# Down-projection products copied out of PSUM and summed in DRAM by adding transfers

## The chip, the cores and the metric

One Trainium2 chip, one of its NeuronCores. The metric is the device time of one execution in microseconds, as the median of several executions; lower is better. The kernel before takes 2646.35 us (median of 3 runs, 2646.03 to 2647.65).

## The reference, cut to what matters

One decoder layer on 512 tokens of width 2048, everything in float32. A mixing stage (a gated linear recurrence beside an RWKV-7 recurrence) is followed by the part that the change touches, a gated feed-forward block with 6144 hidden channels, and then by a gated embedding and a final norm:

```python
u = rmsnorm(h, ln_ffn[i])
gate = causal_dwconv(u @ w_gate[i], conv_f_w[i], conv_f_b[i])     # 512x2048 @ 2048x6144, 3 taps over time
h = h + (jax.nn.gelu(gate) * (u @ w_up[i])) @ w_down[i]           # 512x6144 @ 6144x2048

u = rmsnorm(h, ln_ple[i])
e = jax.nn.sigmoid(u @ w_ple_gate[i]) * (p[i] @ w_ple_proj[i])
h = h + rmsnorm(e, ln_ple_post[i])
return rmsnorm(h, ln_final)
```

## The kernel before, in words

Every large product is done in three passes of a reduced float32 format: each operand is split into a high part, made by a ScalarE copy, and a low part, made by a VectorE subtraction of the high part from the original, and the three products high x high, high x low and low x high are summed in PSUM. Weights arrive through a queue of 512 KB pieces (`wfill_`): SyncE issues the load into a raw buffer (`wraw`, or `hw0` to `hw4` for the down-projection), ScalarE makes `whi` (L127), VectorE makes `wlo` (L128). There are three pairs of `whi` and `wlo`, so a pair is made while TensorE is still at the unit two places ahead of its own. The hidden activations are split by `split` in the same way, high part by ScalarE (L140), low part by VectorE (L141).

`phase2` works through the feed-forward block in 12 chunks of four hidden tiles of 128 channels. For each hidden tile f, `gate_up` runs the gate product and then the up product, in two halves of 24 matmuls each (L1212 to L1214). The gate leaves PSUM by VectorE (L1234), goes through the convolution over time (ScalarE L1236, twice VectorE L1238), the activation (ScalarE L1239) and a scaling on GpSimd (L1240); when the up product is done, VectorE multiplies it in (L1245) into a raw hidden tile (`hw5`, `hw6`). After four tiles, `hidden` forms the chunk's operands.

The down-projection of the first 11 chunks saves an eighth of the multiplications: for each column block b (two of 512 columns in each half of the outputs) it forms seven products i = 0 to 6 of sums of weight quarters and sums of hidden quarters, where plain blocking takes eight. A product is 2 token tiles (tt) by 6 matmuls into two PSUM banks (L1294 to L1296); six banks are shared by these. Its result must be added, with a sign, to one or more of four quarters of the residual stream `h3`, which lies in SBUF as 16 tiles of 128 tokens by 512 columns (number 4 x token tile + column block). In the kernel before, VectorE adds each result straight from PSUM (L1309): to `h3`, or to two running sums in SBUF, `qx` and `qz`, that several quarters share (`ADDS` says which). At the end of the eleventh chunk twenty VectorE additions (L1348) put `qx` and `qz` into `h3`. The last chunk is done by eight plain products (`down_last`, four column blocks, two halves of the hidden channels), added at L1320; after each column block TensorE turns the stream's tiles (`to_features`, L1333) for the next stage. The order of units is written out in `ffn_order`: between products of chunk c stand the gate and up halves of chunk c + 1, so that at the end the last products of chunk 11 lie among the halves of the last hidden tile, f = 47, and `down_last` begins right after its up product.

The instructions of each engine stand in one queue that is fixed at build time. A list scheduler with priorities places them by its own model of durations; at run time each engine takes its queue in order and waits at an instruction until its semaphores are there. The tags of a pool (`T(tag, bufs)`) name buffers that are reused in turn, and an instruction that writes one waits until the last reader of its former content is done.

Of the kernel before, what the change touches and what calls it, by code (L numbers as in the profile page):

```python
# [4 lines left out]
F32 = mybir.dt.float32  # L5
F32R = mybir.dt.float32r
AF = mybir.ActivationFunctionType
ALU = mybir.AluOpType
# [4 lines left out]
S = 512  # L13
# [7 lines left out]
NF = FF // 128  # L21
FC = 4
# [63 lines left out]
class Builder:  # L86
# [1084 lines left out]
    def phase2(self):  # L1171
        nc, A, k2 = self.nc, self.A, self.k2
        V, SC, G, TE = nc.vector, nc.scalar, nc.gpsimd, nc.tensor
        self.MM = 6
        self.auxtag = ("wk", 2)
        T = lambda tag, bufs=1, shape=(128, S), dt=F32: self.t(k2, tag, shape, dt, bufs)
# [22 lines left out]
        h3 = [self.bp.tile([128, S], F32, tag="x%s%d" % ("hl"[i // 8], i % 8), name="h3_%d" % i, bufs=1) for i in range(16)]  # L1199
# [54 lines left out]
        def hidden(last):  # L1254
# [12 lines left out]
            if last:  # L1267
# [14 lines left out]
            return o  # L1282


        qx, qz = (T(n, 1, (128, 2, 2, 512)) for n in ("qx", "qz"))
        st = lambda th, nh: lambda tt, b: h3[(2 * th + tt) * 4 + 2 * nh + b]
        QX, QZ = lambda tt, b: qx[:, tt, b], lambda tt, b: qz[:, tt, b]
        ADDS = [[(QX, ALU.add), (st(0, 0), ALU.add)], [(QZ, ALU.add)], [(QX, ALU.add)], [(st(0, 1), ALU.add)],
                [(st(1, 1), ALU.subtract), (st(1, 0), ALU.add)], [(st(0, 0), ALU.add)], [(st(1, 0), ALU.add)]]

        def product(ps, x, w, tt, first, last):
            ts_ = slice(tt * 128, (tt + 1) * 128)
            for k in range(2):
                TE.matmul(ps, x[0][:, k, ts_], w[0][:, k, :], start=first and k == 0, stop=False)  # L1294
                TE.matmul(ps, x[0][:, k, ts_], w[1][:, k, :], start=False, stop=False)  # L1295
                TE.matmul(ps, x[1][:, k, ts_], w[0][:, k, :], start=False, stop=last and k == 1)  # L1296

        def down(ch, b, i):
            w = self.wnext()
            ps = [self.mm(), self.mm()]  # L1300
            for tt in range(2):
                product(ps[tt], self.hids[ch][i], w, tt, True, True)
            for at, op in ADDS[i]:
                for tt in range(2):
                    o = at(tt, b)
                    if ch == 0 and i < 2 and at in (QX, QZ):
                        SC.activation(o, ps[tt], AF.Copy)
                    else:
                        V.tensor_tensor(o, o, ps[tt], op)  # L1309

        def down_last(cb, kh):
            if kh == 0:
                self.pd = [self.mm() for tt in range(4)]
            w = self.wnext()
            for tt in range(4):
                product(self.pd[tt], self.hids[NF // FC - 1][kh][tt // 2], w, tt % 2, kh == 0, kh == 1)
            if kh == 1:
                for tt in range(4):
                    h = h3[tt * 4 + cb]
                    V.tensor_tensor(h, h, self.pd[tt], ALU.add)  # L1320
# [17 lines left out]
        for o in self.ffn_order():  # L1338
            if o[0] == "g":
                gate_up(*o[1:])  # L1340
            elif o[0] == "q":
                down(*o[1:])
                if o[1:] == (NF // FC - 2, 1, 6):
                    for b in range(2):
                        for q, at, op in ((QX, st(1, 0), ALU.add), (QX, st(0, 1), ALU.subtract), (QZ, st(0, 1), ALU.add),
                                          (QX, st(1, 1), ALU.subtract), (QZ, st(1, 1), ALU.add)):
                            for tt in range(2):
                                V.tensor_tensor(at(tt, b), at(tt, b), q(tt, b), op)  # L1348
            else:
                down_last(*o[1:])  # L1350
                if o[2] == 1:
                    to_features(o[1])
# [13 lines left out]
            self.split(t_[:, 0], t_[:, 1], r)  # L1366
            px.append((t_[:, 0], t_[:, 1]))
        rsh = k2.tile([128, 4], F32, name="rsh")
        hq = [T("q" + n, 1, (128, 2, 512)) for n in "xz"]
        ss = k2.tile([128, 20], F32, name="ss")  # L1370

        sg2, sb = (k2.tile([128, 20], F32, name=n) for n in ("sg2", "sb"))
        se, sge, sbe, ssh = (k2.tile([128, 4], F32, name=n) for n in ("se", "sge", "sbe", "ssh"))
        MU, AD = ALU.mult, ALU.add
# [80 lines left out]
        for cb in range(4):  # L1455
            ph, pl = self.wnext()
            p2 = [T("hw%d" % (6 + i), 1, (128, 2, 512)) for i in range(2)]
            pp = [p2[tt // 2][:, tt % 2] for tt in range(4)]
            for tt in range(4):
                ps = self.mm()  # L1460
                ts_ = slice(tt * 128, (tt + 1) * 128)
                for k in range(2):
                    TE.matmul(ps, px[k][0][:, ts_], ph[:, k, :], start=k == 0, stop=False)
                    TE.matmul(ps, px[k][0][:, ts_], pl[:, k, :], start=False, stop=False)
                    TE.matmul(ps, px[k][1][:, ts_], ph[:, k, :], start=False, stop=k == 1)
                SC.activation(pp[tt], ps, AF.Copy)
            if cb == 0:
                t_ = k2.tile([128, 4], F32, name="rsp")
                V.tensor_reduce(ssh.unsqueeze(2), ss3.rearrange("p (t c) -> p t c", c=4), mybir.AxisListType.X, ALU.add)
                V.tensor_scalar(t_, ssh, 1.0 / D, RMS_EPS, ALU.mult, ALU.add)  # L1470
                G.tensor_tensor(t_, t_, self.mhalf[:, 0:4], ALU.pow)
                V.tensor_scalar(rsh, t_, 0.5, None, ALU.mult)
            n, w = (8, 512) if cb < 3 else (4, 256)
            pg = [self.mm()[:, 0:w] for tt in range(4)]
            for u in range(n):
                kk = KT // n
                gate(pg, range(4), [self.wnext()], range(u * kk, u * kk + kk), u == 0, u == n - 1)
                if cb == 3 and u == 1:
                    us = [self.wnext(), self.wnext()]
            for tt in range(4):  # L1480
                embed(tt, cb, gated(tt, pg[tt], slice(0, w)), pp, slice(0, w))
                post(tt, cb, slice(0, w))
                if cb == 3:

                    SC.activation(hq[tt // 2][:, tt % 2, 0:256], h3[tt * 4 + 3][:, 256:512], AF.Copy)
                    V.tensor_tensor(pp[tt][:, 0:256], pp[tt][:, 256:512], gpost[3][:, 256:512], MU)
                gain(tt, cb)
        early()
# [3 lines left out]
        with self.tc.manual_schedule(engines={ET.PE, ET.DVE, ET.Activation, ET.Pool}):  # L1492
            for tt in range(4):
                pg = {tt: self.mm()[:, 0:256]}
                for u in range(5):
                    if u == len(us):
                        us.append(self.wnext())
                    k = 2 * u if u < 2 else 4 * u - 4
                    gate(pg, [tt], us[u:u + 1], range(k, KT), u == 0, u == 4)

                sg, ee, x = T("tmp", 2), T("tmp", 2), e[tt * 4 + 3][:, last]
                n5 = slice(tt * 5 + 4, tt * 5 + 5)
                SC.activation(sg[:, last], pg[tt], AF.Tanh, scale=rsh[:, tt:tt + 1])
                V.scalar_tensor_tensor(ee[:, last], sg[:, last], 1.0, pp[tt][:, last], AD, MU)
                SC.activation(ee[:, last], ee[:, last], AF.Square, accum_out=ss[:, n5])
                V.scalar_tensor_tensor(x, sg[:, last], 1.0, pp[tt][:, 0:256], AD, MU)
                SC.activation(sg[:, 0:256], x, AF.Square, accum_out=sg2[:, n5])
                V.scalar_tensor_tensor(ee[:, 0:256], hq[tt // 2][:, tt % 2, 0:256], 2.0, x, MU, MU, accum_out=sb[:, n5])
# [12 lines left out]
            for cb in range(4):  # L1521
                final(3, rf, cb, cb < 3)
# [67 lines left out]
```

## Time and profile before

| | |
|---|---|
| Time, median of 3 runs | 2646.35 us |
| Lowest and highest | 2646.03 and 2647.65 us |
| Span of the profiled execution, first to last instruction | 2643.4 us |
| What lies around it (median less span) | 2.95 us |
| TensorE matmuls busy | 2601.4 us, 98% of the span |
| VectorE busy | 1721.3 us, 65% |
| ScalarE busy | 1081.7 us, 41% |
| GpSimd busy | 219.4 us, 8% |
| Moved by DMA | 265.56 MB, 100 GB/s in the mean |
| Mean granted TensorE clock | 0.993 |

Busy shares are means over the whole span. Matmuls overlap each other in the pipeline, so a busy TensorE isn't yet one at its peak, but where it is busy in every slice no other engine can delay it there. All transfers of this kernel are issued by SyncE; GpSimd issues none, so this trace holds no row of its queue. In the rows, PE is TensorE, PEld its weight load, DVE is VectorE, ACT ScalarE, POOL GpSimd and SP SyncE; SPq is SyncE's issue of a transfer.

### The profile page before, as it was taken

To read this page: it belongs to the slowest core of one execution; us is meant where nothing else is said; L and a number is where in the kernel's file an instruction comes from. 1 tells how busy PE (TensorE), PEld (TensorE's weight loads), DVE (VectorE), ACT (ScalarE), POOL (GpSimd) and SP (SyncE) were. 2 spreads that over 40 slices of the span, in tenths; PEclk is the share of its full clock that TensorE was granted. 3 is DMA by queue.
4 is the path that set the end of the run, shared out by engine and by line. 5 is a ranking of instruction groups with operands and counts; after the bars stand their busy time and mean duration, and the time that the engine had idled before them with its cause. 6 is when DMAs were issued, how large, how long until landed. Compare 5 with 4: busy or idle time off the path is not lost.

```text
span 2643.4 us, 43548 instructions
## 1 busy us (share of the span) xinstructions
PE 2601.4 (98%) x18466; PEld 2133.7 (81%) x18466; DVE 1721.3 (65%) x2420; ACT 1081.7 (41%) x1515; POOL 219.4 (8%) x177
## 2 busy tenths in 40 slices
PE   9989999999999999999999999999999999999997
PEld 8867778777877888888888888888888888888887
DVE  5764776667666535666676676666666667775447
ACT  6563555546433433333333333333333333335335
POOL 0010000101122300000000000000000000000001
PEclk9999999999999999999999999999999999999999
DMA  7222222222243323223232323323332332332223
GB/s 250 92 69 66 93 77 68 79 79 90 93 129 128 105 87 104 96 97 110 97 104 94 106 95 101 107 96 106 101 105 97 103 104 96 104 108 88 96 92 108
DMA packets 84483, 265.56 MB, mean 100 GB/s; under 512 B 9792, under 2 KB 12480, under 8 KB 84288
## 3 DMA queue, kind: packets, MB, share of 16 engines
q1 hardware_dynamic: 84288, 262.78, 30.1%
q8 instruction: 144, 2.36, 0.4%
q14 instruction: 51, 0.42, 0.1%
HBM read 254.62 MB, written 8.13 MB: 99 GB/s over the span
## 4 chain that ended last, share of the span: by engine, by line
PE 69%; DVE 2%; ACT 1%; issue 1%; POOL 0%; DMA 0%; POOLq 0%; ACTq 0%; DVEq 0%
PE wk L1212 12%; PE wk L1213 12%; PE wk L1214 12%; PE mm L1296 6%; PE mm L1295 6%; PE mm L1294 6%; PE mm L1385 2%; PE mm L1387 2%; PE mm L1386 2%; PE mm L157 2%; PE mm L161 2%; PE mm L159 2%; PE mm L1212 1%; PE mm L1214 1%; PE mm L1213 1%
## 5 line engine op out<-in xcount | busy, mean ns | idle before, releaser
L127 ACT ACTIVATE whi<-wraw 128x1024 fp32r<-128x1024 f32 (+1 forms) x361 | 373.8, 1035 | 746.9 <-PE mm L159 205.8
L128 DVE TENSOR_TENSOR wlo<-wraw,whi 128x1024 fp32r<-128x1024 f32 (+1 forms) x361 | 440.5, 1220 | 207.6 <-ACT whi L127 201.6
L1212 PE MATMUL wk<-uh,whi 128*128 128x512 f32 x1408 | 547.8, 389 | 0.0
L1213 PE MATMUL wk<-ul,whi 128*128 128x512 f32 x1408 | 547.7, 389 | 0.0
L1214 PE MATMUL wk<-uh,wlo 128*128 128x512 f32 x1408 | 547.7, 389 | 0.0
L127 ACT ACTIVATE whi<-hw 128x1024 fp32r<-128x1024 f32 x154 | 163.3, 1061 | 464.6 <-PE wk L1213 414.4
L157 PE MATMUL mm<-xh,whi 128*128 128x512 f32 x832 | 332.6, 400 | 0.9 <-DVE hT L447 0.9
L161 PE MATMUL mm<-xh,wlo 128*128 128x512 f32 x832 | 332.5, 400 | 0.0
L159 PE MATMUL mm<-xl,whi 128*128 128x512 f32 x832 | 330.9, 398 | 0.0
L1214 PEld LDWEIGHTS wk<-uh,wlo 128*128 128x128 f32 x1408 | 264.4, 188 | 54.8
L1212 PEld LDWEIGHTS wk<-uh,whi 128*128 128x128 f32 x1408 | 264.4, 188 | 54.7
L1213 PEld LDWEIGHTS wk<-ul,whi 128*128 128x128 f32 x1408 | 264.4, 188 | 54.7
L128 DVE TENSOR_TENSOR wlo<-hw,whi 128x1024 fp32r<-128x1024 f32 x154 | 188.7, 1225 | 181.5 <-ACT whi L127 179.1
L1295 PE MATMUL mm<-wlo,hid 128*128 128x512 f32 x680 | 265.1, 390 | 0.0
L1296 PE MATMUL mm<-whi,hid 128*128 128x512 f32 x680 | 264.9, 390 | 0.0
L1294 PE MATMUL mm<-whi,hid 128*128 128x512 f32 x680 | 264.8, 389 | 0.0
L1240 POOL TENSOR_TENSOR tmp<-tmp,rsa 128x512 f32<-128x512 f32 x48 | 87.2, 1818 | 1361.1 <-ACT tmp L1239 1361.1
L157 PEld LDWEIGHTS mm<-xh,whi 128*128 128x128 f32 x832 | 157.4, 189 | 36.4 <-issue 3.0
L161 PEld LDWEIGHTS mm<-xh,wlo 128*128 128x128 f32 x832 | 157.2, 189 | 34.4 <-issue 1.9
L159 PEld LDWEIGHTS mm<-xl,whi 128*128 128x128 f32 x832 | 157.3, 189 | 33.7 <-issue 1.8
L1309 DVE TENSOR_TENSOR h<-h,mm 128x512 f32<-128x512 f32 x264 | 175.0, 681 | 0.6
L1295 PEld LDWEIGHTS mm<-wlo,hid 128*128 128x128 f32 x680 | 127.7, 188 | 26.3
(514 smaller groups left out, 3592.1 us busy)
## 6 DMA issues: line engine op xcount, KB each, us to landing
wraw<-wgu SPq DMA_DIRECT2D x192, 512.0 KB, 3.2
hw<-wd SPq DMA_DIRECT2D x88, 512.0 KB, 3.3
wraw<-wz SPq DMA_DIRECT2D x80, 512.0 KB, 3.6
wraw<-wpg SPq DMA_DIRECT2D x31, 512.0 KB, 3.2
wraw<-wo SPq DMA_DIRECT2D x22, 512.0 KB, 3.4
wraw<-wo SPq DMA_DIRECT2D x20, 256.0 KB, 3.0
tmp<-xT SPq DMA_DIRECT2D x16, 256.0 KB, 2.7
wraw<-wd SPq DMA_DIRECT2D x8, 512.0 KB, 3.2
```

Of the source, the lines that this page charges most:

```text
L127: nc.scalar.activation(hi, raw, AF.Copy)
L128: nc.vector.tensor_tensor(lo, raw, hi.bitcast(F32), ALU.subtract)
L157: nc.tensor.matmul(ps, hi[:, k, :], xh, start=first and i == 0, stop=False)
L159: nc.tensor.matmul(ps, hi[:, k, :], xl, start=False, stop=False)
L161: nc.tensor.matmul(ps, lo[:, k, :], xh, start=False, stop=last and i == n - 1)
L1212: TE.matmul(ps, wh[:, k, :], xh, start=h + k == 0, stop=False)
L1213: TE.matmul(ps, wh[:, k, :], xl, start=False, stop=False)
L1214: TE.matmul(ps, wl[:, k, :], xh, start=False, stop=h == 1 and k == 7)
L1294: TE.matmul(ps, x[0][:, k, ts_], w[0][:, k, :], start=first and k == 0, stop=False)
L1295: TE.matmul(ps, x[0][:, k, ts_], w[1][:, k, :], start=False, stop=False)
L1296: TE.matmul(ps, x[1][:, k, ts_], w[0][:, k, :], start=False, stop=last and k == 1)
L1309: V.tensor_tensor(o, o, ps[tt], op)
```

## The change

The two running sums are gone. Each product now has partial sums of its own in DRAM: 28 tiles `pacc`, one for each product i, token tile tt and column block b. ScalarE copies every product from PSUM into one of 8 SBUF buffers `pl` (L1321), and GpSimd's queue sends it to DRAM, for the first chunk as a plain store (L1323), after that as a transfer that adds to what is there (L1325): 308 copies and 308 transfers. For each column block b a new function `combine` loads the 14 partial sums back on GpSimd's queue (L1293), again into `pl` buffers, and VectorE joins them to the stream in 22 additions (L1289). `combine(0)` is called in the eleventh chunk after product 3 of column block 1, `combine(1)` after product 6, the last. The `pl` buffers take the room that `qx` and `qz` had; four of them hold the copies `hq` later on.

```diff
-        qx, qz = (T(n, 1, (128, 2, 2, 512)) for n in ("qx", "qz"))
-        st = lambda th, nh: lambda tt, b: h3[(2 * th + tt) * 4 + 2 * nh + b]
-        QX, QZ = lambda tt, b: qx[:, tt, b], lambda tt, b: qz[:, tt, b]
-        ADDS = [[(QX, ALU.add), (st(0, 0), ALU.add)], [(QZ, ALU.add)], [(QX, ALU.add)], [(st(0, 1), ALU.add)],
-                [(st(1, 1), ALU.subtract), (st(1, 0), ALU.add)], [(st(0, 0), ALU.add)], [(st(1, 0), ALU.add)]]
+        pacc = [[[self.dp.tile([128, S], F32, name="pacc%d_%d_%d" % (i, tt, b)) for b in range(2)] for tt in range(2)] for i in range(7)]
+        st = lambda th, nh, tt, b: h3[(2 * th + tt) * 4 + 2 * nh + b]
+
+        def combine(b):
+            add = lambda o, x, op=ALU.add: V.tensor_tensor(o, o, x, op)
+            for tt in range(2):
+                p = [T("pl", 8) for i in range(7)]
+                for i in (0, 2, 5, 1, 4, 6, 3):
+                    nc.gpsimd.dma_start(p[i], pacc[i][tt][b])
+                c00, c10, c01, c11 = (st(th, nh, tt, b) for nh in range(2) for th in range(2))
+                add(c00, p[0])
+                add(c00, p[5])
+                add(p[0], p[2])
+                add(p[1], p[0], ALU.subtract)
+                add(c10, p[4])
+                add(c10, p[6])
+                add(c10, p[0])
+                add(c01, p[3])
+                add(c01, p[1])
+                add(c11, p[4], ALU.subtract)
+                add(c11, p[1])
...
-            for at, op in ADDS[i]:
-                for tt in range(2):
-                    o = at(tt, b)
-                    if ch == 0 and i < 2 and at in (QX, QZ):
-                        SC.activation(o, ps[tt], AF.Copy)
-                    else:
-                        V.tensor_tensor(o, o, ps[tt], op)
+            for tt in range(2):
+                o = T("pl", 8)
+                SC.activation(o, ps[tt], AF.Copy)
+                if ch == 0:
+                    G.dma_start(pacc[i][tt][b], o)
+                else:
+                    G.dma_start(pacc[i][tt][b], o, accum_op=ALU.add)
...
                 down(*o[1:])
+                if o[1:] == (NF // FC - 2, 1, 3):
+                    combine(0)
                 if o[1:] == (NF // FC - 2, 1, 6):
-                    for b in range(2):
-                        for q, at, op in ((QX, st(1, 0), ALU.add), (QX, st(0, 1), ALU.subtract), (QZ, st(0, 1), ALU.add),
-                                          (QX, st(1, 1), ALU.subtract), (QZ, st(1, 1), ALU.add)):
-                            for tt in range(2):
-                                V.tensor_tensor(at(tt, b), at(tt, b), q(tt, b), op)
+                    combine(1)
...
-        hq = [T("q" + n, 1, (128, 2, 512)) for n in "xz"]
+        hq = [T("pl", 8) for tt in range(4)]
```

Up to the end of the first chunk's gate and up products the queues of all engines are the same. What the scheduler makes of the end of the block is shown at four places. In these rows a name is followed by a number that tells its uses apart, `h` is a tile of the stream, `mm` and `wk` are PSUM banks, `par` holds convolution weights.

VectorE, from the last multiplication of the up product (L1245, tile f = 47) to the low parts of the last two hidden operands (L141, `hid`). Before:

```order
L1348 TENSOR_TENSOR h_13_10678<-h_13_10678,qx_10681 128x512
L1245 TENSOR_TENSOR hw_3207_20658<-tmp_20765,wk_20792 128x512
L128 TENSOR_TENSOR wlo_20919<-wraw_20916,whi_20918 128x1024
L141 TENSOR_TENSOR hid_20905<-hw_3207_20658,hid_20904 128x512
L141 TENSOR_TENSOR hid_20909<-hw_3207_20658,hid_20908 128x512
L128 TENSOR_TENSOR wlo_20949<-wraw_20946,whi_20948 128x1024
```

After, the end of that stretch; between L1245 and the first row here stand two weight splits and ten further additions of L1289:

```order
L1289 TENSOR_TENSOR h_13_10678<-h_13_10678,pl_21478 128x512
L1289 TENSOR_TENSOR h_5_10670<-h_5_10670,pl_21479 128x512
L1289 TENSOR_TENSOR pl_21474<-pl_21474,pl_21476 128x512
L1289 TENSOR_TENSOR h_13_10678<-h_13_10678,pl_21480 128x512
L1289 TENSOR_TENSOR pl_21475<-pl_21475,pl_21474 128x512
L1289 TENSOR_TENSOR h_13_10678<-h_13_10678,pl_21474 128x512
L1289 TENSOR_TENSOR h_7_10672<-h_7_10672,pl_21477 128x512
L1289 TENSOR_TENSOR h_15_10680<-h_15_10680,pl_21478 128x512
L1289 TENSOR_TENSOR h_7_10672<-h_7_10672,pl_21475 128x512
L1289 TENSOR_TENSOR h_15_10680<-h_15_10680,pl_21475 128x512
L141 TENSOR_TENSOR hid_21539<-hw_3505_21198,hid_21538 128x512
L141 TENSOR_TENSOR hid_21543<-hw_3505_21198,hid_21542 128x512
```

Before, one weight split stands between L1245 and the two L141; now two weight splits and all but two of `combine(1)`'s 22 additions do.

GpSimd, after, where `combine(0)` begins (before, there is no row at all between the scalings of tiles 46 and 47). In `pacc` the three numbers are token tile, column block and a serial number; the product's own number isn't printed:

```order
L1293 DMA pl_21225<-pacc_0_0_10681 128x512
L1325 DMA pacc_1_1_10696<-pl_21222 128x512
L1293 DMA pl_21227<-pacc_0_0_10689 128x512
L1293 DMA pl_21230<-pacc_0_0_10701 128x512
L1293 DMA pl_21226<-pacc_0_0_10685 128x512
L1293 DMA pl_21229<-pacc_0_0_10697 128x512
L1293 DMA pl_21231<-pacc_0_0_10705 128x512
L1293 DMA pl_21228<-pacc_0_0_10693 128x512
L1293 DMA pl_21250<-pacc_1_0_10683 128x512
L1293 DMA pl_21252<-pacc_1_0_10691 128x512
L1293 DMA pl_21255<-pacc_1_0_10703 128x512
L1293 DMA pl_21251<-pacc_1_0_10687 128x512
```

The first row loads the partial sum 0 of the first token tile, the third to eighth the products 2, 5, 1, 4, 6 and 3; then comes the second token tile with its products 0, 2, 5 and 1 (its 4, 6 and 3 follow). Seven loads of a token tile take seven of the eight `pl` buffers. So of the second token tile only the load of partial sum 0 has a buffer that no addition must free first; its partial sum p takes the buffer that p - 1 of the first token tile had, and the load stands in the queue until the last addition that reads that one is done. The next copies of products (`pl_21324` and those after it in the ScalarE rows below) take the buffers of the second token tile in the same way, and the loads of `combine(1)` those of these copies and of each other.

GpSimd, around the scaling of tile f = 47 (L1240). Before, the queue holds nothing but such scalings and, after them, small powers:

```order
L1240 TENSOR_TENSOR tmp_20304<-tmp_20304,rsa 128x512
L1240 TENSOR_TENSOR tmp_20524<-tmp_20524,rsa 128x512
L1240 TENSOR_TENSOR tmp_20765<-tmp_20765,rsa 128x512
L1471 TENSOR_TENSOR rsp<-rsp,mhalf 128x4
L1418 TENSOR_TENSOR tl_22792<-tl_22790,mhalf 128x1
```

After:

```order
L1325 DMA pacc_0_1_10706<-pl_21443 128x512
L1293 DMA pl_21449<-pacc_0_1_10682 128x512
L1325 DMA pacc_1_1_10708<-pl_21446 128x512
L1293 DMA pl_21451<-pacc_0_1_10690 128x512
L1293 DMA pl_21454<-pacc_0_1_10702 128x512
L1240 TENSOR_TENSOR tmp_21361<-tmp_21361,rsa 128x512
L1293 DMA pl_21450<-pacc_0_1_10686 128x512
L1293 DMA pl_21453<-pacc_0_1_10698 128x512
L1293 DMA pl_21455<-pacc_0_1_10706 128x512
L1293 DMA pl_21452<-pacc_0_1_10694 128x512
L1293 DMA pl_21474<-pacc_1_1_10684 128x512
```

The scaling now stands behind the store of the very last product (the third row) and two loads; eleven loads follow it, of which five are shown.

ScalarE, at the same tile's convolution and activation (L1236, L1239). Before:

```order
L1236 ACTIVATE tmp_20765<-row_10663,par 128x512
L140 ACTIVATE hw_3357_21374<-ld_21372 128x512
L127 ACTIVATE whi_20795<-wraw_20793 128x1024
L1239 ACTIVATE tmp_20765<-tmp_20765 128x512
L127 ACTIVATE whi_20825<-wraw_20823 128x1024
```

After:

```order
L1321 ACTIVATE pl_21324<-mm_21310 128x512
L140 ACTIVATE hw_3691_22008<-ld_22006 128x512
L127 ACTIVATE whi_21395<-wraw_21393 128x1024
L1321 ACTIVATE pl_21327<-mm_21311 128x512
L1321 ACTIVATE pl_21386<-mm_21372 128x512
L1321 ACTIVATE pl_21389<-mm_21373 128x512
L127 ACTIVATE whi_21425<-wraw_21423 128x1024
L1321 ACTIVATE pl_21443<-mm_21429 128x512
L1236 ACTIVATE tmp_21361<-row_10663,par 128x512
L127 ACTIVATE whi_21501<-wraw_21499 128x1024
L1321 ACTIVATE pl_21446<-mm_21430 128x512
L1239 ACTIVATE tmp_21361<-tmp_21361 128x512
```

The copies of the products 4, 5 and 6 of the last chunk's second column block (six `pl` rows) now stand between the weight splits. The copy of the very last one (`pl_21446`, which the GpSimd store above sends) stands behind this tile's L1236, and so behind the VectorE instruction L1234 that L1236 reads.

More of the change, by code (lines that the diff above doesn't have):

```diff
@@ L1483, in phase2 @@
                 if cb == 3:
-                    SC.activation(hq[tt // 2][:, tt % 2, 0:256], h3[tt * 4 + 3][:, 256:512], AF.Copy)
+                    SC.activation(hq[tt][:, 0:256], h3[tt * 4 + 3][:, 256:512], AF.Copy)
                     V.tensor_tensor(pp[tt][:, 0:256], pp[tt][:, 256:512], gpost[3][:, 256:512], MU)
@@ L1507, in phase2 @@
                 SC.activation(sg[:, 0:256], x, AF.Square, accum_out=sg2[:, n5])
-                V.scalar_tensor_tensor(ee[:, 0:256], hq[tt // 2][:, tt % 2, 0:256], 2.0, x, MU, MU, accum_out=sb[:, n5])
+                V.scalar_tensor_tensor(ee[:, 0:256], hq[tt][:, 0:256], 2.0, x, MU, MU, accum_out=sb[:, n5])
                 V.tensor_tensor(x, x, gfin[3][:, last], MU)
```

## The prediction

> **What bounds the kernel now.** I read the page first, then the windows by stage, the list of waits, and the rows of every engine at the end of the feed-forward block. The page's totals, TensorE's waits after 770 us (engine, producer: us, times, longest), and one window from the last short waits to the end of TensorE's dense work (busy time of PE, PEld, DVE, ACT and POOL, granted clock, DMA share, GB/s):
>
> ```profile
> PE 2601.4 (98%) x18466; PEld 2133.7 (81%) x18466; DVE 1721.3 (65%) x2420; ACT 1081.7 (41%) x1515; POOL 219.4 (8%) x177
> ...
> PE mm L157 <- DVE hT L447: 0.9, 1, 0.9
> ...
> 900.00:2620.00 1720.00, 1720.00 (x7808) 1430.94 (x7807) 1111.03 (x1362) 602.79 (x753) 95.35 (x54) 1.00 0.29 99
> ```
>
> TensorE is busy for all of these 1720 us, at full clock, and waits for nobody. The change leaves the matmuls as they are. So whatever it takes off VectorE is worth nothing; at most the 0.9 us of that one wait could be won. And any stall put into this window moves the end by its own length.
>
> TensorE's own times at the end of the block (start, us of one matmul): the units of 12 matmuls of a product (L1294) and of 24 of a gate or up half (L1212).
>
> ```profile
> 2335.82 0.39 PE L1294 MATMUL mm<-whi,hid 128*128 128x512 f32 x1
> 2343.97 0.39 PE L1294 MATMUL mm<-whi,hid 128*128 128x512 f32 x1
> 2346.70 0.39 PE L1212 MATMUL wk<-uh,whi 128*128 128x512 f32 x1
> 2376.61 0.39 PE L1294 MATMUL mm<-whi,hid 128*128 128x512 f32 x1
> 2387.50 0.82 PE L1333 MATMUL wk<-con,h 128*128 128x128 f32 x6
> ```
>
> A product and a half take 8.15 us (2335.82 to 2343.97), so a matmul 0.2264 to 0.2268 us: 12 are 2.72, 24 are 5.44. Product 3 of column block 1 ends at 2346.70. After it: half, product 4 (from 2352.14), half (2354.86), product 5 (2360.30), half of the up product (2363.0), product 6 (2368.45), half (2371.2), `down_last` from 2376.61. Of `down_last` the scheduler now puts 48 matmuls first that need no low part of the last hidden operands: TensorE asks for that low part (L141) at 2376.61 + 48 x 0.2268 = 2387.50. That is the appointment which matters.
>
> **Steady state, eleven chunks: nothing.** The groups (count | busy us, mean ns | idle) of the additions out of PSUM and of a ScalarE copy out of PSUM, and the weight split that stands behind such work:
>
> ```profile
> L1309 DVE TENSOR_TENSOR h<-h,mm 128x512 f32<-128x512 f32 x264 | 175.0, 681 | 0.6
> L1309 DVE TENSOR_TENSOR qx<-qx,mm 128x512 f32<-128x512 f32 x84 | 57.0, 682 | 0.3
> L1309 DVE TENSOR_TENSOR qz<-qz,mm 128x512 f32<-128x512 f32 x40 | 25.5, 677 | 0.0
> ...
> 2346.89 1.06 ACT L127 ACTIVATE whi<-wraw 128x1024 fp32r<-128x1024 f32 x1 [1.88 <-DVE h L1309]
> ...
> 2348.10 1.22 DVE L128 TENSOR_TENSOR wlo<-wraw,whi 128x1024 fp32r<-128x1024 f32 x1
> 2349.24 0.69 DVE L1348 TENSOR_TENSOR h<-h,qx 128x512 f32<-128x512 f32 x1
> ...
> 2357.89 1.29 DVE L1348 TENSOR_TENSOR h<-h,qx 128x512 f32<-128x512 f32 x2
> 2359.09 1.29 DVE L1348 TENSOR_TENSOR h<-h,qz 128x512 f32<-128x512 f32 x2
> ...
> L1307 ACT ACTIVATE qx<-mm x4: 577/580/598, 1023.6 to 1077.9; 128x512 f32<-128x512 f32 x4
> ```
>
> VectorE loses 388 additions (L1309) and 20 (L1348), each 0.60 apart (two from 2357.89 to 2359.09), and gets 44 (L1289): some 218 us less, on an engine that nobody waits for. ScalarE gets 308 copies for 8, by 0.58 us 174 us more: two in 8.15 us. The pair split at 2348.10 to 2349.24 is for the half that starts at 2354.86: 5.6 us of cover, and two copies are 1.2. If that cover were gone, TensorE would wait by what goes beyond.
>
> GpSimd gets 308 transfers of 256 KB, two in 8.15 us. No row shows its issue. Bounds per transfer, a: SyncE's issue from below, GpSimd's own pass over such a tile from above (a row of L1245 stands here too); SyncE's loads of the same 256 KB from DRAM (KB, median us from issue to landing) give the rest of the way:
>
> ```profile
> 2367.38 0.33 SPq L1364 DMA_DIRECT2D ld<-pT  x1
> ...
> 2365.25 1.55 POOL L1240 TENSOR_TENSOR tmp<-tmp,rsa 128x512 f32<-128x512 f32 x1 [33.81 <-ACT tmp L1239]
> ...
> 2376.89 0.69 DVE L1245 TENSOR_TENSOR hw<-tmp,wk 128x512 f32<-128x512 f32 x1 [1.96 <-PE wk L1214]
> ...
> lx<-oa SPq DMA_DIRECT2D x3, 256.0 KB, 2.7
> row<-oa SPq DMA_DIRECT2D x3, 256.0 KB, 2.9
> ```
>
> a lies between 0.33 and 1.55; neither row is nearer in kind (one is an issue by another engine, the other no issue at all), so I take the middle, 0.94. Landing after the issue: 2.8 less 0.33, 2.5 us. A `pl` buffer is then back 0.58 + 0.94 + 2.5 = 4 us after its copy begins; eight buffers are four products, 32.6 us. DMA's share, 0.29, rises: 64 GB/s of stores and as much read back, at the window's 99 GB/s for 0.29, is about 0.38 more. The scaling L1240 now stands behind transfers; it ended at 2366.80 and is read by L1245 at 2376.89: 10 us of cover against two issues, 1.9. None of the three shows on TensorE.
>
> **The end of the block: four round trips.** What the additions need must be loaded, into buffers that the additions themselves free. The rows of before for the instructions on the way:
>
> ```profile
> 2360.49 0.69 DVE L1234 TENSOR_TENSOR row<-wk,rsa 128x512 f32<-128x512 f32 x1
> 2361.28 0.81 ACT L1236 ACTIVATE tmp<-row,par 128x512 f32<-128x512 f32 x1
> ...
> 2377.68 1.23 DVE L128 TENSOR_TENSOR wlo<-wraw,whi 128x1024 fp32r<-128x1024 f32 x1
> 2378.82 1.28 DVE L141 TENSOR_TENSOR hid<-hw,hid 128x512 fp32r<-128x512 f32 x2
> ...
> 2377.61 1.15 ACT L140 ACTIVATE hid<-hw 128x512 fp32r<-128x512 f32 x2
> ```
>
> A split counts 1.14 (2377.68 to 2378.82), an addition 0.60.
>
> 1. `combine(0)`, first token tile. Weight split 2346.89 + 1.06, copy 0.58: product 3 leaves at 2348.53. GpSimd sends it and issues the loads of partial sums 2 and 5: 3a, 2351.35; landed 2353.85. From there VectorE has nine additions (the third to the eleventh) and two splits, 5.40 + 2.28: 2361.53. The later loads arrive under these.
> 2. Second token tile. Its loads wait for buffers, the first of them for that last addition. Loads 2, 5, 1, 4: 4a, and 2.5: 2367.79. Ten additions and two splits, 6.00 + 2.28: 2376.07. The splits belong to product 6, wanted at 2368.45 and ready at 2369.53, and to the half behind it: TensorE waits 1.1 and 0.2, and would begin `down_last` at 2377.9.
> 3. Only now do ScalarE's next copies have a buffer, and only now comes L1234 (2360.49 before). ScalarE: two copies 1.16, split of `down_last`'s first weights 1.06: 2378.29; VectorE's half 1.14: TensorE begins at 2379.43, 1.5 late. ScalarE goes on: copy 0.58, L1236 0.81, split 1.06, copy of the last product 0.58: 2381.32. GpSimd: store and two loads 3a, then L1240 1.55: 2385.69 (2366.80 before). The second load lands at 2385.70, one addition, L1245 0.69, the high parts 1.15: 2388.14, where TensorE, after 24 matmuls, has waited 3.3.
> 4. `combine(1)`. Loads 1, 4, 6, 3 stand behind L1240: 4a and 2.5, 2391.95; four additions and a split 3.54: 2395.49. This frees the second tile's buffers: 4a and 2.5, 2401.75; ten additions 6.0 and L141 1.28: 2409.03.
>
> Against the appointment at 2387.50 that is 21.5 us; the smaller waits above are contained in it, and the last one is about 13 us.
>
> What a wait of TensorE costs beyond itself shows earlier in the trace (windows as above; the row before them has the idle time in brackets):
>
> ```profile
> 188.46 0.48 PE L772 MATMUL wk<-AR,ktl 64*64 64x128 f32 x2 [5.21 <-DVE ktl L705]
> ...
> 186.80:188.40 1.60, 0.00 (x0) 0.00 (x0) 1.60 (x1) 0.00 (x0) 1.06 (x1) 0.50 0.55 223
> 188.40:193.80 5.40, 5.34 (x37) 4.24 (x37) 2.01 (x4) 2.91 (x6) 0.11 (x1) 0.54 0.02 3
> 193.80:196.00 2.20, 2.20 (x45) 1.65 (x44) 0.93 (x3) 0.00 (x0) 0.00 (x0) 1.00 0.00 0
> ```
>
> Idle from 183.25, the clock stood at 0.50 by 186.8, and at 0.54 for 5.4 us after work had begun again: 5.4 x 0.46 = 2.5 us lost. The 13 us wait brings that once; the waits of up to 3.3 us are shorter than the 3.5 us after which it is seen.
>
> The sum stands on the profiled execution, whose span 2643.4 and 2.95 around it are the median of 2646.35: 2646.35 + 21.5 + 2.5 = **2670.3**. Bounds, the same walk: a = 0.33 gives 13.4, with the clock 2662.2; a = 1.55 gives 35.5, with two losses of clock (product 6 then waits 6.8 us too) 2686.9.
>
> The Trainium skill, "TensorE: Matmul & The Clock Gate", Part 1: The HAM clock gate, halves the rate after an idle window of about 3.4 us and restores it after about 3.4 us of sustained work; the fall agrees with the row, the return took longer here. By the page 1.7 us would stand for 2.5, and the sum would be 2669.6. Its "DMA: Bandwidth & Descriptors", Anatomy of one DMA — SWDGE (gpsimd) path, gives 2.0 us + bytes / 436e3, for 256 KB 2.6 us in all, an estimate that leaves 1.7 us behind an issue of 0.94; no row of GpSimd's queue can confirm it here. By it the walk gives 18.3 and the sum 2667.2.
>
> **Rivals.**
> - *GpSimd's issue is slow* (a of 1.2 and more, or landings near 4 us beside the weight loads). For it: the engine's pass over 256 KB takes 1.55. Against: it need not touch the data. 27 to 35 us and one or two clock losses: 2676 to 2687. Chance 0.18.
> - *It is cheap as SyncE's* (a below 0.5): 13.4 to 15 and 2.5, 2662 to 2664. Chance 0.12.
> - *The queue bounds the steady state.* An adding transfer reads and writes DRAM; the share leaves room, but no row shows one. It decides from 8.15 / 2 = 4.08 us per transfer; at 5 us each of 140 later products costs 1.85 more: 259 us, 2905. Chance 0.05.
> - *Not slower: the sums cost nothing.* If the transfers were all hidden, VectorE's own queue would still hold twenty additions and two splits between L1245 and L141; the walk with free transfers ends 6.5 us late, with the clock 9.0, 2655.4. It takes additions of 0.50 us as well, and a clock that holds, to come to 4.0 us, 2650.4. The quoted additions, 0.60 apart, speak against it. Chance 0.05, of it 0.02 for a gain.
>
> **Numbers.** My forecast (a of 0.5 to 1.2: 15 to 26 us, 2664 to 2675) has the remaining 0.60; the time is its middle. From 2660 to 2687 lies this, nearly all of the first rival and most of the second. 0.2% is 5.3 us, about what a measurement tells from no change: slower 0.95, same 0.03, faster 0.02.
>
> **What would show it.** PE stays at 200 of 200 us in windows before 2340. Near its end an idle stretch of about 13 us before a matmul of L1312, released by VectorE's L141, with the clock at a half behind it, and one of about 3 before `down_last`'s L1310. L1289's idle time is put down to DMA, in four clusters; L1234 of the last tile starts near 2376 and L1240 ends near 2386. GpSimd's issue near 0.94 us. I am wrong if TensorE waits in earlier chunks (a copy of ScalarE, a `pl` buffer), if L1289 never waits for a load, or if the time lies at one place that the walk doesn't pass.

## The result: 2871 us, and the profile after

| | before | after |
|---|---|---|
| Time, median | 2647.0 us | 2871.39 us (2862.16 to 2878.46) |
| Ratio | | 1.0848, 95% interval 1.0829 to 1.0866 |
| Span of the profiled execution | 2643.4 us | 2873.7 us |
| TensorE busy | 2601.4 us | 2641.7 us |
| TensorE's waits after 900 us | none | 189.7 us |

The kernel became 224 us slower. The range of the prediction ended at 2687. The engines' totals on the page:

```profile
PE 2641.7 (92%) x18466; PEld 2153.6 (75%) x18466; DVE 1504.6 (52%) x2056; ACT 1232.8 (43%) x1815; POOL 471.2 (16%) x513
```

The list of TensorE's waits from 900 us on (us in total, times, longest):

```profile
PE wk L1212 <- DVE hw L1245: 127.1, 9, 18.2
PE mm L1311 <- DVE wlo L128: 30.1, 4, 23.2
PE mm L1310 <- ACT hid L140: 17.6, 1, 17.6
PE mm L1312 <- DVE hid L141: 9.7, 1, 9.7
PE wk L1214 <- DVE wlo L128: 5.2, 9, 0.6
```

Two windows of the feed-forward block (busy time of PE, PEld, DVE, ACT and POOL, clock, DMA share, GB/s), around the first chunk with its plain stores, and most of the chunks with adding ones:

```profile
1000.00:1200.00 200.00, 200.00 (x889) 165.76 (x888) 104.35 (x107) 88.80 (x119) 34.46 (x44) 1.00 0.51 148
1200.00:2300.00 1100.00, 977.64 (x4201) 801.11 (x4200) 486.05 (x499) 422.89 (x558) 228.84 (x246) 0.94 0.65 138
```

The waits come to 189.7 us. Besides them TensorE is busy 40.3 us longer for the same 18466 matmuls, because its clock was lowered after each long wait (0.94 granted in the second window, 1.00 before). After thirteen waits of 3.9 us and more the matmuls stood 0.43 us apart in place of 0.23 for 3.1 to 7.9 us; these stretches come to 77.5 us, half of which is 38.8. Waits and longer work together are 230.0 us, against 230.3 us between the spans. Of the waits 127.1 us are nine of 9 to 18 us, each in a later chunk and each on the multiplication L1245; the others stand at the end of the block.

One of the nine, by the rows of GpSimd, ScalarE, VectorE and TensorE (start, us, instruction, idle time before it and what ended it):

```profile
1366.85 0.90 POOL L1325 DMA_DIRECT2D pacc<-pl  x1 [2.18 <-issue]
...
1404.12 0.87 POOL L1325 DMA_DIRECT2D pacc<-pl  x1 [3.32 <-issue]
1408.45 0.86 POOL L1325 DMA_DIRECT2D pacc<-pl  x1 [3.46 <-issue]
1412.91 0.87 POOL L1325 DMA_DIRECT2D pacc<-pl  x1 [3.59 <-issue]
1417.39 0.86 POOL L1325 DMA_DIRECT2D pacc<-pl  x1 [3.61 <-issue]
1417.97 1.58 POOL L1240 TENSOR_TENSOR tmp<-tmp,rsa 128x512 f32<-128x512 f32 x1
...
1385.31 0.62 ACT L1239 ACTIVATE tmp<-tmp 128x512 f32<-128x512 f32 x1
...
1419.58 0.69 DVE L1245 TENSOR_TENSOR hw<-tmp,wk 128x512 f32<-128x512 f32 x1 [26.90 <-POOL tmp L1240]
...
1420.42 0.77 PE L1212 MATMUL wk<-uh,whi 128*128 128x512 f32 x1 [15.83 <-DVE hw L1245]
```

The activation (L1239) was ready at 1385.93. Its scaling L1240 started at 1417.97, 32 us later: eleven adding transfers stand ahead of it in GpSimd's queue (1366.85 to 1417.39, 5.05 us apart in the mean and 4.2 to 4.5 in the last rows), and seven of them were still to be issued when it was ready. Each issue took 0.87 us; in the 3.3 to 3.6 us ahead of it the engine waited for nothing that the profile shows ("issue"). The gap is the finding of this case. In the first chunk, with plain stores, there is none. The groups of GpSimd's issues (count | busy us, mean ns | idle and what ended it):

```profile
L1325 POOL DMA_DIRECT2D pacc<-pl x280 | 245.5, 877 | 1082.0 <-issue 593.6 <-ACT pl L1321 210.8 <-ACT whi L127 171.9
L1293 POOL DMA_DIRECT2D pl<-pacc x28 | 15.9, 568 | 21.7 <-issue 13.3 <-DVE h L1289 7.4 <-DVE hw L1245 0.4
L1323 POOL DMA_DIRECT2D pacc<-pl x28 | 15.5, 554 | 80.9 <-ACT pl L1321 80.9
```

GpSimd's DMA queue (packets, MB, share of 16 engines), and the median way of its stores (KB, us from issue to landing):

```profile
q0 software_dynamic: 44800, 88.10, 20.9%
...
pacc<-pl POOLq DMA_DIRECT2D x308, 256.0 KB, 4.2
```

The 28 plain stores waited for their copies alone. The 280 adding ones waited 593.6 us for nothing named, and their pitch (the time from one issue to the next) is about their landing, 4.2 us: as if each went only when the one before was done.

### The profile page after: what moved, and what is told of

It reads as the page before. It is cut to its first block, busy times and chain, and to the rows that moved or that the text cites. A ratio compares the mean times of both kernels' runs of the same rounds, so it can differ in the third digit from the quotient of the medians.

```text
span 2873.7 us, 44316 instructions
## 1 busy us (share of the span) xinstructions
PE 2641.7 (92%) x18466; PEld 2153.6 (75%) x18466; DVE 1504.6 (52%) x2056; ACT 1232.8 (43%) x1815; POOL 471.2 (16%) x513
## 3 DMA queue, kind: packets, MB, share of 16 engines
q0 software_dynamic: 44800, 88.10, 20.9%
## 4 chain that ended last, share of the span: by engine, by line
PE 46%; issue 19%; POOL 5%; DVE 3%; ACT 1%; DMA 1%; POOLq 0%; ACTq 0%; DVEq 0%
PE wk L1214 7%; PE wk L1212 7%; PE wk L1213 7%; PE mm L1312 4%; PE mm L1311 4%; PE mm L1310 4%; POOL pacc L1325 4%; PE mm L1399 2%; PE mm L1401 2%; PE mm L1400 2%; PE mm L157 2%; PE mm L161 2%; PE mm L159 2%; POOL tmp L1240 1%; PE mm L1212 1%
## 5 line engine op out<-in xcount | busy, mean ns | idle before, releaser
L1212 PE MATMUL wk<-uh,whi 128*128 128x512 f32 x1408 | 559.2, 397 | 127.1 <-DVE hw L1245 127.1
L1214 PE MATMUL wk<-uh,wlo 128*128 128x512 f32 x1408 | 557.9, 396 | 5.2 <-DVE wlo L128 5.2
L1213 PE MATMUL wk<-ul,whi 128*128 128x512 f32 x1408 | 556.9, 396 | 0.0
L1325 POOL DMA_DIRECT2D pacc<-pl x280 | 245.5, 877 | 1082.0 <-issue 593.6
L1212 PEld LDWEIGHTS wk<-uh,whi 128*128 128x128 f32 x1408 | 270.7, 192 | 186.8 <-issue 130.6
L1213 PEld LDWEIGHTS wk<-ul,whi 128*128 128x128 f32 x1408 | 270.4, 192 | 56.7
L1311 PE MATMUL mm<-wlo,hid 128*128 128x512 f32 x680 | 269.3, 396 | 30.1 <-DVE wlo L128 30.1
L1310 PE MATMUL mm<-whi,hid 128*128 128x512 f32 x680 | 268.6, 395 | 17.6 <-ACT hid L140 17.6
L1312 PE MATMUL mm<-whi,hid 128*128 128x512 f32 x680 | 267.4, 394 | 9.7 <-DVE hid L141 9.7
L1321 ACT ACTIVATE pl<-mm 128x512 f32<-128x512 f32 x308 | 179.0, 589 | 142.7 <-DMA pacc<-pl 64.4
L1245 DVE TENSOR_TENSOR hw<-tmp,wk 128x512 f32<-128x512 f32 x44 | 30.2, 686 | 356.0 <-POOL tmp L1240 320.4
```

The source lines that it names most:

```text
L1212: TE.matmul(ps, wh[:, k, :], xh, start=h + k == 0, stop=False)
L1213: TE.matmul(ps, wh[:, k, :], xl, start=False, stop=False)
L1214: TE.matmul(ps, wl[:, k, :], xh, start=False, stop=h == 1 and k == 7)
L1325: G.dma_start(pacc[i][tt][b], o, accum_op=ALU.add)
```

## The experiments

Times are single runs where no interval is given; the kernel before took 2651.1 us beside e1 to e4, 2646.3 beside m1 to m3 and e5, 2644.9 beside e6 and e7. Over all these runs it lay between 2640.5 and 2651.1, so a few us between two single runs mean nothing.

**What makes the gap: room, adding, sharing, or the place of L1240.** The second run, e2, has more room and one `pl` buffer fewer; e1, with the old room and seven buffers, is the control for it. The edit of e1 (a third such line, for `hq`, is left out):

```diff
-                p = [T("pl", 8) for i in range(7)]
+                p = [T("pl", 7) for i in range(7)]
...
-                o = T("pl", 8)
+                o = T("pl", 7)
```

> A control for the next run: seven pl buffers in place of eight, nothing else. In the changed kernel GpSimd's adding transfers follow each other every 4.4 us (issue 0.87, then 3.3 to 3.9 of nothing that the profile shows), and TensorE's waits in the feed-forward block come to 190 us. All theories put the limit into that pitch and not into the number of buffers: 2860 to 2890 us, pitch unchanged.

Measured: 2867.8 us, within the 2862 to 2878 of eight buffers. The number of buffers is not it. The edit of e2, on top of that:

```diff
-    nc = _bacc.Bacc("TRN2", target_bir_lowering=False, num_devices=1, dynamic_dma_scratch_size=512)
+    nc = _bacc.Bacc("TRN2", target_bir_lowering=False, num_devices=1, dynamic_dma_scratch_size=2048)
```

> Seven pl buffers, and the room that the build reserves for GpSimd's descriptors is 2048 bytes a partition in place of 512 (L1597; with eight buffers it doesn't fit into SBUF). Theory A (room): an adding transfer makes 144 packets, a plain one 80, and only one adding transfer at a time has room, so that the next issue waits until it has landed (pitch 4.4 us against a landing of 4.2). Then the pitch falls below 2 us where copies are ready, TensorE no longer waits in the middle of the block, and only the end of the block costs, by the walk of the prediction some 20 to 30 us: 2660 to 2690 us. Theory B (adding transfers follow one another whatever room there is, each behind the one before): nothing changes, 2860 to 2890 us.

Measured: 2668.22 us. Against e1, 200 us are gone by this one number. GpSimd's group of adding transfers:

```profile
L1325 POOL DMA_DIRECT2D pacc<-pl x280 | 243.7, 914 | 723.3 <-ACT pl L1321 723.2
```

TensorE's waits after 900 us:

```profile
PE mm L1312 <- DVE hid L141: 8.6, 1, 8.6
PE mm L1310 <- ACT hid L140: 7.5, 1, 7.5
PE mm L1399 <- ACT tmp L1406: 0.3, 1, 0.3
```

The long window:

```profile
1200.00:2300.00 1100.00, 1100.00 (x4854) 911.21 (x4854) 573.93 (x575) 492.02 (x645) 277.16 (x281) 1.00 0.71 160
```

The unnamed gap has vanished, every wait of the queue is for a copy, and TensorE is busy for all 1100 us, with DMA's share higher than before (0.71). Theory A stands, B falls.

The next two runs start from the changed kernel again, with its eight buffers and 512 bytes of room. The edit of e3:

```diff
-                    G.dma_start(pacc[i][tt][b], o, accum_op=ALU.add)
+                    G.dma_start(pacc[i][tt][b], o)
```

> All 308 transfers are plain stores; nothing is summed in DRAM, so the loads at the end bring only the last chunk's products. Bytes written, issues, waits and buffers are the same; left out are the adding and the reading back that it needs. Theories A and B: the cost goes with the adding; a plain store issues in 0.55 us and three followed each other without a gap in the first chunk. TensorE waits only at the end of the block: 2660 to 2690 us. Theory C (the writes and the weight loads share the DMA engines, whose busy share rose from 0.30 to 0.67): most of the loss stays, above 2800 us.

Measured: 2671.03 us. The same group, now of plain stores:

```profile
L1325 POOL DMA_DIRECT2D pacc<-pl x280 | 153.3, 548 | 800.2 <-ACT pl L1321 797.0 <-issue 2.6
```

The queue's line for the same bytes:

```profile
q0 software_dynamic: 26880, 88.10, 9.2%
```

Theory C falls, and by e2 too, where all engines' share is higher still. The queue's line also shows what an adding transfer is made of: 336 plain ones, loads among them, make 26880 packets, 80 each; in the changed kernel 44800 packets are 56 plain ones of 80 and 280 adding ones of 144.

The edit of e4:

```diff
-                G.tensor_tensor(c, c, rs, ALU.mult)
+                V.tensor_tensor(c, c, rs, ALU.mult)
```

> The scaling of the activation (L1240) is done by VectorE, so nothing that TensorE waits for stands in GpSimd's queue behind transfers. A chunk is 14 products and 16 halves of 2.72 and 5.44 us, 125 us, and has 28 transfers of 4.4 us, 123 us. Theory D (place): the queue has just capacity enough over a chunk, and the loss comes from L1240 standing behind up to five late transfers; then TensorE's waits for L1245 vanish and 2680 to 2720 us remain, with the end of the block dearer than in the prediction. Theory E (capacity): the copies on ScalarE then wait for pl buffers, the weight splits behind them come late, and 2800 us or more remain.

Measured: 2793.45 us; theory E was the nearer. The nine waits for L1245 are gone, so the place of L1240 did carry them, but the queue is too slow by itself. Two issues of it, the second the 33rd after the first with nothing else between:

```profile
1601.84 0.87 POOL L1325 DMA_DIRECT2D pacc<-pl  x1 [3.64 <-issue]
...
1759.74 0.88 POOL L1325 DMA_DIRECT2D pacc<-pl  x1 [4.08 <-issue]
```

The two largest entries of TensorE's waits:

```profile
PE mm L1311 <- DVE wlo L128: 42.1, 3, 37.0
PE wk L1212 <- ACT whi L127: 29.3, 27, 4.4
```

157.9 us / 33 = 4.78 us. A chunk's 28 transfers take 134 us, and TensorE's work in a chunk 125. The waits for `whi` of over 1 us come back every 133 to 136 us. So ScalarE's copies wait for buffers (466.7 us in 162 waits for a transfer out of `pl`; in e2 0.2 us), the splits behind them come late (29.3 us in 27 pieces), and what is left over comes due at the end of the block: there the first addition of `combine(0)` waited 33.8 us for its load, with the weight split behind it that TensorE waited 37.0 us for.

**The gap by itself.** Three kernels that compute nothing of the layer: from GpSimd's queue twelve plain stores of a tile, then twelve adding transfers.

```python
for i in range(N):
    nc.gpsimd.dma_start(a[i], s1)
...
for i in range(N):
    nc.gpsimd.dma_start(b[i], s2, accum_op=ALU.add)
```

> The disputed cost by itself, nothing of the layer is computed: twelve plain stores of one 128x512 tile from GpSimd's queue to twelve tiles in DRAM, all ready at once, and later twelve adding transfers in the same way; room 512 bytes a partition as in the changed kernel. Theory A (room for one adding transfer): the adding ones issue every 4.2 to 4.5 us, as in the full kernel, though no other traffic runs; of the plain ones the first three issue 0.55 us apart, then one per 1 to 2 us. Theory C (the pitch comes from sharing the DMA engines with weight loads): without that traffic the pitch falls clearly below 4 us.

> The same with 1024 bytes a partition. Theory A: a second or third adding transfer fits (144 packets each, 9 per DMA engine): two or three issue 0.9 us apart, then one per 1.5 to 2.5 us. Theory B (each behind the one before): 4.2 to 4.5 us as before.

> The same with 2048 bytes a partition. Theory A: five or more adding transfers issue 0.9 us apart before the first gap, and then the pitch is that of the DMA engines: 1.8 us by the busy share of the changed kernel's software queue (20.9% of 2873.7 us for 336 transfers).

Measured, first the rows of m1 (512 bytes), then of m2 (1024), then of m3 (2048); `x3` is three instructions without a gap between them:

```profile
33.53 1.79 POOL L42 DMA_DIRECT2D plain<-one  x3 [33.09 <-DVE one L40]
36.31 0.55 POOL L42 DMA_DIRECT2D plain<-one  x1 [0.99 <-issue]
...
47.40 0.54 POOL L42 DMA_DIRECT2D plain<-one  x1 [0.53 <-issue]
56.53 0.89 POOL L50 DMA_DIRECT2D added<-two  x1 [8.59 <-DVE two L48]
60.79 0.88 POOL L50 DMA_DIRECT2D added<-two  x1 [3.37 <-issue]
...
104.37 0.86 POOL L50 DMA_DIRECT2D added<-two  x1 [3.55 <-issue]
```

```profile
33.64 5.51 POOL L42 DMA_DIRECT2D plain<-one  x10 [33.20 <-DVE one L40]
...
54.53 2.68 POOL L50 DMA_DIRECT2D added<-two  x3 [13.07 <-DVE two L48]
58.99 0.84 POOL L50 DMA_DIRECT2D added<-two  x1 [1.78 <-issue]
...
72.99 0.85 POOL L50 DMA_DIRECT2D added<-two  x1 [1.40 <-issue]
```

```profile
33.20 6.56 POOL L42 DMA_DIRECT2D plain<-one  x12 [32.76 <-DVE one L40]
54.15 7.95 POOL L50 DMA_DIRECT2D added<-two  x9 [14.38 <-DVE two L48]
62.41 0.86 POOL L50 DMA_DIRECT2D added<-two  x1 [0.31 <-issue]
```

With 512 bytes one adding transfer goes at a time, (104.37 - 56.53) / 11 = 4.35 us apart with no other traffic, which is 0.3 us more than its median from issue to landing:

```profile
added<-two POOLq DMA_DIRECT2D x12, 256.0 KB, 4.0
```

With 1024 three are issued without a gap and then one per 1.75 us (58.99 to 72.99, eight steps); with 2048 nine. Of the plain ones three, ten and all twelve are issued without a gap. Expected was this order, and the numbers for 512; for 2048 the guess of 1.8 us after the burst was too long: the last three issues are 1.2 us apart, and one transfer landed every 1.3 us (60.73 to 73.56, ten steps).

A burst without a gap isn't yet the number that are under way, because its first transfers land before its last is issued. By the landings in these traces the most that were under way together were one, three and seven adding transfers, and three, seven and (with none held back) eight plain ones. Every issue that was held back began 0.25 to 0.4 us after a landing. The limit counts packets: 3 x 80 = 240 went with 512 bytes and 2 x 144 = 288 did not, 7 x 80 = 560 with 1024 and 4 x 144 = 576 did not, 7 x 144 = 1008 with 2048 and 8 x 144 = 1152 did not. A limit on the number of transfers would be the same for both kinds.

**Fewer and larger transfers in the same room.** On the changed kernel; the plain stores of the first chunk and the loads of `combine` are changed to match:

```diff
-            for tt in range(2):
-                o = T("pl", 8)
-                SC.activation(o, ps[tt], AF.Copy)
...
+            o = T("pl", 4, (128, 2, 512))
+            for tt in range(2):
+                SC.activation(o[:, tt, :], ps[tt], AF.Copy)
...
+                G.dma_start(pacc[i][b], o, accum_op=ALU.add)
```

> Room 512 and the same bytes, but one transfer of 512 KB for a product (both token tiles, four buffers of double size) in place of two of 256 KB: 14 in a chunk. If what is limited is the number of transfers in flight, the pitch is about 5 us and 70 of a chunk's 125 us: TensorE waits only at the block's end, 2665 to 2695 us. If it is the number of packets, 256 and more for such a transfer, the pitch doubles to some 8 to 9 us: 2830 us or more, as before.

Measured: 2678.51 us, TensorE busy for all 1100 us from 1200 to 2300, with 512 bytes of room. The long window, the queue's line and the median way:

```profile
1200.00:2300.00 1100.00, 1100.00 (x4855) 910.84 (x4854) 573.75 (x576) 490.56 (x643) 170.76 (x158) 1.00 0.68 159
...
q0 software_dynamic: 24416, 88.09, 18.8%
...
pacc<-pl POOLq DMA_DIRECT2D x154, 512.0 KB, 5.7
```

24416 packets are 154 transfers of 144 (the 14 plain ones of the first chunk made 2016) and 28 loads of 80: an adding transfer of 512 KB has as many packets as one of 256 KB, and not the 256 and more of the guess. So this run can't tell a limit on packets from one on transfers; m1 to m3 can. Landing takes 5.7 us in place of 4.2, for twice the bytes.

**What is left: the end of the block.** Two more edits on top of e2, first that of e6:

```diff
                 down(*o[1:])
-                if o[1:] == (NF // FC - 2, 1, 3):
-                    combine(0)
-                if o[1:] == (NF // FC - 2, 1, 6):
-                    combine(1)
```

> Room 2048, seven buffers, and no combine at all: the partial sums are never loaded and never added to the stream (that part of the result is left out). It prices what is left of the loss in e2. Theory F (the end of the block is the four round trips of the prediction, and the copies, transfers and DMA's busy share of 0.7 cost TensorE nothing): the time is that of the kernel before, 2645 to 2652 us, and TensorE waits for nothing after 900 us. Theory G (part of the 17 us that remain in e2 is contention spread over the block): 2655 us or more.

Measured over three rounds: ratio to before 1.0007, interval 0.9997 to 1.0016; median 2646.48 us. TensorE waits for nothing between 900 and 2640 us; the window up to 2620:

```profile
900.00:2620.00 1720.00, 1720.00 (x7805) 1430.47 (x7805) 878.49 (x953) 756.67 (x1053) 350.65 (x362) 1.00 0.61 146
```

VectorE's busy time in this window fell from 1111 to 878 us, ScalarE's rose from 603 to 757, DMA's share doubled, and the time is the same. What e2 lost beyond the kernel before lies in the combines: theory F. The edit of e7:

```diff
-                if o[1:] == (NF // FC - 2, 1, 3):
+                if o[1:] == (NF // FC - 2, 0, 6):
                     combine(0)
-                if o[1:] == (NF // FC - 2, 1, 6):
-                    combine(1)
             else:
                 down_last(*o[1:])
                 if o[2] == 1:
                     to_features(o[1])
+                    if o[1] == 0:
+                        combine(1)
```

> Room 2048, seven buffers, and the two combines where they are first possible or still early enough: combine(0) after product 6 of column block 0, combine(1) after the first column block has been turned for the next stage (to_features(0)); the low parts of the last hidden operands then stand ahead of combine(1)'s additions but for two. Theory F: the four trips no longer stand ahead of what TensorE asks for; 2647 to 2657 us. Rival: the trips are as long as before and only arrive elsewhere, since L1234 and L1336 now stand among the additions; 2660 us or more.

Measured: ratio 1.0049, interval 1.0032 to 1.0067 (2657.23 us, before 2644.9 in the same rounds): just past the upper edge of what F expected, and below the rival's 2660. The wait for the low parts (L1312) is gone. Five waits of under 1 us and one of 4.4 us remain; the latter comes because two additions of `combine(1)` still stand ahead of L1245 on VectorE:

```profile
2389.22 0.69 DVE L1289 TENSOR_TENSOR pl<-pl,pl 128x512 f32<-128x512 f32 x1 [3.02 <-DMA pl<-pacc]
2389.83 0.68 DVE L1245 TENSOR_TENSOR hw<-tmp,wk 128x512 f32<-128x512 f32 x1
...
2391.23 0.80 PE L1310 MATMUL mm<-whi,hid 128*128 128x512 f32 x1 [4.36 <-ACT hid L140]
```

No version beats the kernel before, and by e6 this design has nothing to gain: without any combine it just reaches the same time.

## Why the prediction was wrong, step by step

- **The step that failed: "GpSimd gets 308 transfers of 256 KB, two in 8.15 us", priced by their issue.** The issue itself was well guessed: a = 0.94 forecast, 0.87 measured for adding transfers (0.55 for plain stores and loads). But the queue's price of an adding transfer was taken to be its issue, 1.9 us in 8.15, with landings free to overlap. With the room that this build reserves they could not: the price was the whole way from issue to landing and 0.3 us more, 4.35 us with no other traffic and 4.78 in the full kernel (e4). Everything that the prediction put under cover by this step failed with it: the 10 us ahead of L1240 were asked to cover not two issues but, at the place shown, seven whole transfers, and a `pl` buffer was not back in 4 us.
- **The rival that came about was written down, at 0.05.** It named the queue as the bound and priced 5 us per transfer at 2905 us; 4.78 and 2871 were measured. Its mechanism was not the right one (DRAM read and written at once: e2 moves the same bytes through the same adding at 2668 us), and its threshold was a little strict: 4.08 us is the pair of a product and a half, but a chunk has 125 us for 28 transfers, 4.47 each. The chance was too small for a queue of which the trace showed no row at all; 0.33 and 1.55 bounded an issue, not a pitch.
- **ScalarE's copies, VectorE's relief, DMA's share: nothing, right where the queue is free.** e6 shows all three at once. The share was forecast at 0.29 + 0.38 = 0.67; 0.65 was measured in the long window, 0.71 where the queue ran freely.
- **The four round trips: right in size, where the queue is free, and that partly by luck.** The walk gave 21.5 us and 2.5 for the clock, 24.0. e2's span is 2666.5 us, 23.1 above that of before; 2.3 of these were there ahead of the block's end (the L1245 of the tile before the last starts at 2346.56 for 2344.24), which leaves 20.8. Against the kernel before measured beside it, one run each, it is 17.1. The two waits are those that the walk named, for the high parts (L1310) and for the low parts (L1312), but they are 7.5 and 8.6 us. The walk had 3.3 for the first; for the second it said 13, though 21.5 less its other waits leaves 15.4. The last L1245 came later than in the walk (2390.62 for 2386.30; the loads landed after 5.5 us in the median, not after 0.94 and 2.5), and what stands behind it came faster, so that L141 began at 2407.30 for 2407.75. The walk's lower bound, 13.4 us for a = 0.33, doesn't follow from its steps as printed: eighteen issues, 0.61 us shorter each, give 10.5. e1 to e3 can't tell the trips from each other; e6 shows their sum. In the changed kernel itself the queue's backlog arrives here too: 17.6 and 9.7 us, and 23.2 for a weight split (L1311) that stands on VectorE behind an addition that waited 24.6 us for its load.
- **The clock: one loss forecast, two came.** The walk took one loss of 2.5 us, for the 13 us, and none for waits of up to 3.3 us. In e2 both waits brought one: the matmuls, 0.43 us apart at first, came back to 0.23 about 3.1 us after the wait of 7.5 us and 4.3 us after that of 8.6, which at half the pace is 3.7 us lost. In e5 a wait of 3.1 us was enough (0.50 granted from 2380.3 to 2383.4). In the changed kernel the return took 3.1 to 7.9 us, so neither the 5.4 us of the prediction's row nor one shorter figure holds for all. The Trainium skill, "TensorE: Matmul & The Clock Gate", Part 1: The HAM clock gate, gives about 3.4 us of sustained work; the first return in e2 is near it, most of those in the changed kernel are longer.
- **The way of one transfer.** Beside weight loads a plain store took 3.1 us in the median (e3), and an adding one 4.0 even in m1, where they went one at a time. The Trainium skill, "DMA: Bandwidth & Descriptors", Anatomy of one DMA — SWDGE (gpsimd) path, has a fit by which 256 KB take 2.6 us, an estimate; a plain store that is alone agrees with it (the first of m1, m2 and m3 landed after 2.5 us each), an adding one does not.

## What to carry to other kernels

A transfer costs a queue two different things, its issue and its turn: if a queue that no trace of yours has shown is to carry a steady load, bound its pitch by the landing, not by the issue alone, and hold that against the work of a whole period. Put nothing that others wait for into a queue of transfers that may block, least of all an instruction that is ready long before. Where the queue blocks, more room for it or fewer, larger transfers of the same bytes gave back 200 and 193 us, and moving the waiting instruction elsewhere only 78.

## What the runs showed of the hardware

- The room that the build reserves for GpSimd's transfers (512, 1024, 2048 bytes a partition) let one, three and seven adding transfers of 256 KB be under way at once, and three, seven and at least eight plain ones (m1 to m3). When it is full, GpSimd itself stands still, and a scaling that was ready stood 32 us behind such transfers (the changed kernel).
- An adding transfer of a 128x512 float32 tile has 144 packets and issues in 0.87 us, a plain one 80 and 0.55 us. One of 128x1024 has 144 as well (e5).
- Adding alone is not slow: with room for seven, adding transfers landed every 1.3 us in m3, each 8.6 us after its issue in the median, where one at a time landed after 4.0 us but only every 4.35.
- After a wait TensorE's full clock came back within 3.1 to 7.9 us, and a wait of 3.1 us was enough to lose it (the changed kernel, e5).
